# First gather of the experts as one run through four accumulator banks; gates by one product per token block

## The chip, the cores and the metric

The kernel runs on one core of one Trainium2 chip. The metric is the time on the device in microseconds of one execution. Five engines work side by side, each through its own list in its own order: TensorE (PE: matrix products; PEld is its weight load), VectorE (DVE), ScalarE (ACT), GpSimd (POOL) and SyncE (SP), which here issues the large transfers. They wait for each other by semaphores. PE writes its products into PSUM, of which this kernel uses eight pieces of 128 partitions by 2 KB, called banks here; DVE and ACT read them out into SBUF.

## What is computed

A transformer of two layers on one sequence of 256 tokens of width 1024, all in float32. Each layer is a token mixer (four kinds of attention, gated and merged), a layer norm, a mixture of 32 experts, and a second layer norm. The change lies in the mixture:

```
scores = sigmoid(x @ w_router)                     # 256 tokens, 32 experts in 8 groups of 4
g_sel  = group with the largest sum of its two best (score + bias)
e_idx  = the two best experts inside that group;  gate = their scores, normalised to sum 1
for every expert e, for the tokens sent to it:
    hid = silu(x @ w1[e]) * (x @ w3[e])            # 1024 -> 256
    y  += gate * (hid @ w2[e])                     # 256 -> 1024
x = layer_norm(ALPHA * x + y)
```

Each layer reads 32 experts of 3 MB, some 100 MB of weights.

## The kernel before

The mixture of layer `l` runs after a router. Tokens get a place in a table of 64 slots for each pair of experts; a `OH` matrix (one-hot, 256 tokens by 256 slots, made by DVE at L1260) says which token sits in which slot, for two steps of the loop at once. The main loop runs over `q` = 0 to 7 (`NQ`), and in it over `s` = 0 and 1: one `head` is a pair of experts side by side (`i` = 0, 1, each 64 slots, on the two halves of the PE columns), for `j` = 0 to 7, the eight slices of 128 of the width.

The steps that matter, with their lines:

- `gather` (L1299 to L1309): for each slice `j`, four products of x (as a high and a low part, two token blocks) with `OH` give the 256 gathered slots of that slice in PSUM, 128 by 256. DVE (L1309, even `j`) or ACT (L1307, odd `j`) scales them into `xg[:, j, :]`. Each `j` takes a PSUM tile of its own, a bank each, of a tag ("h" or "y", two banks each) that is used in turn.
- `head` (L1317): for each `j`, two products with w1 and w3 of the two experts, 64 rows by 512 columns each. The trace has two records for each product, so a head is 32 records.
- `hidden` (L1324 to L1326), `flip` (L1332 to L1334), `tail` (L1354, products with w2, read out by ACT at L1348 and DVE at L1349), `combine` (L1398 and L1394, sums into the four accumulator banks `acc`).
- `gates_of` (L1366 to L1369): the gate of each slot as a column, by a product of the one-hot with the gates of the tokens; called twice at each even `q`, after `flip_key` (L1376, read by DVE at L1379).

The first gather of a layer is special. It is interleaved with the first head: slice `j` is gathered, and from the third on the head's slice `j - 2` follows it (`GL = 2`), through the "y" banks alone. The last two slices of that head come in the loop. All later gathers run as one piece of 32 products, with "h" and "y" in turn.

The order on PE inside the loop is the order in which the code is written (`manual_schedule`); DVE, ACT and POOL are placed by the scheduler of the framework. Expert weights come through a ring of 20 slots of 1 MB (`SLOTS`), filled by SP in the order of use; a slot is loaded again when PE has finished with what it held (L1007 and L1023 issue the transfers).

Of the kernel before, what the change touches and what calls it, by code (L numbers as in the profile page):

```python
# [10 lines left out]
F32 = mybir.dt.float32  # L11
# [22 lines left out]

DS = 4
NX = 8
GL = 2
OUT_CUT = 896
HOLD = 2

# [62 lines left out]
def build(ctx, tc, I, consts, out, dbg=None, layers=L):  # L103
    nc = tc.nc
    pe, act, dve, pool = nc.tensor, nc.scalar, nc.vector, nc.gpsimd
# [12 lines left out]
    def a8(dims, dt=F32):  # L118
        t = mx.tile([128, 2048], dt, name="a8", bufs=2)
        return t.rearrange("p (a b) -> p a b", b=dims[-1])  # L120
# [251 lines left out]
    for l in range(layers):  # L372
# [25 lines left out]
        with ExitStack() as mst:  # L398
# [550 lines left out]
            for hp, u in enumerate((37 - DS, 43 - DS)):  # L949
                held, pair = {}, [None, None]  # L950
                for hh in range(2):
                    h = 2 * hp + hh
# [41 lines left out]
            a13s, a2s = {}, {}  # L994
# [40 lines left out]
            def load_ahead(n):  # L1035

                while loads and cnt[0] < n:
                    with tc.issue_after(last_load[0]):
                        loads.pop(0)()

            def release(n):
                cnt[1] += n
                load_ahead(cnt[1] + len(SLOTS))
# [16 lines left out]
            def wo_piece(n, j0):  # L1060
                return split(wos(n * 256, 256)[:, j0:j0 + 2], 2, S)
# [18 lines left out]
            with tc.issue_after(mcopy.ins):  # L1080
                for i, wt in ((1, wrb), (0, wrg[0])):
                    o = 72 + 16 * i + 8 * l
# [53 lines left out]
            for n in range(3):  # L1136
                ps = mp.tile([128, 2, S], F32, name="pj")
                for j0 in range(0, 8, 2):
                    h, lo = wop.pop(j0) if n == 0 and j0 in wop else wo_piece(n, j0)
# [7 lines left out]
            for tb in range(2):  # L1147
                ts_ = slice(tb * 128, tb * 128 + 128)
                ps = mp.tile([128, S], F32, name="pj")
                for j in range(8):  # L1150
                    if tb and j in ROUTE0:
                        route_last(0, ROUTE0.index(j))
                    h, lo = pieces[j // 2]
# [87 lines left out]
            for tb in range(2):  # L1241
                pe.matmul(prk[:, :, NP:], oneb, osel[:, tb, None, 0:NP].to_broadcast([128, 2, NP]), start=False, stop=False,
                          skip_group_check=True)
# [10 lines left out]
            G = 256  # L1254
# [12 lines left out]
            ohs = {0: oh0}  # L1267
# [16 lines left out]
            for i in range(2):  # L1284
                H = slice(64 * i, 64 * i + 64)
# [7 lines left out]
        with ExitStack() as ost:  # L1293
# [2 lines left out]

            op = ost.enter_context(tc.tile_pool(name=f"op{l}", bufs=2, space=PSUM))

            def gather(xg, oh, js, g, tags="hy"):  # L1299

                for j in js:
                    px = op.tile([128, g], F32, name=tags[j % 2])
                    for i, (xx, tb) in enumerate(((x1h, 0), (x1l, 0), (x1h, 1), (x1l, 1))):
                        pe.matmul(px, xx[:, tb, j, :], oh[:, tb, :], start=(i == 0), stop=(i == 3))  # L1304
                    g_, b_ = gpj[:, 0, l, j:j + 1], gpj[:, 1, l, j:j + 1]
                    if j % 2:
                        act.activation(xg[:, j, :], px, AF.Identity, scale=g_, bias=b_)  # L1307
                    else:
                        dve.tensor_scalar(xg[:, j, :], px, g_, b_, op0=OP.mult, op1=OP.add)  # L1309

            def head(xs, a13, ph=None, js=range(8)):

                if ph is None:
                    ph = op.tile([128, 2, 256], F32, name="h")
                for j in js:
                    for i in range(2):
                        pe.matmul(ph[64 * i:64 * i + 64], xs(j, i), a13[i][j], start=(j == 0), stop=(j == 7),  # L1317
                                  skip_group_check=True)
                return ph

            def hidden(ph, m):

                th = mx.tile([128, 256], F32, name="th", bufs=2)
                act.activation(th, ph[:, 0, :], AF.Tanh, scale=0.5)  # L1324
                dve.scalar_tensor_tensor(th, th, 1.0, ph[:, 0, :], op0=OP.add, op1=OP.mult)  # L1325
                dve.scalar_tensor_tensor(th, th, m, ph[:, 1, :], op0=OP.mult, op1=OP.mult)  # L1326
                return th
# [32 lines left out]

            def gates_of(oh, g):

                gp = op.tile([128, 1], F32, name="y")
                for tb in range(2):
                    for i in range(2):
                        pe.matmul(gp[64 * i:64 * i + 64], oh[:, tb, 64 * i:64 * i + 64].bitcast(F32), g[:, tb, i:i + 1],  # L1366
                                  start=(tb == 0), stop=(tb == 1), skip_group_check=True)
                gcol = mx.tile([128, 1], F32, name="gcol", bufs=4)
                dve.tensor_copy(gcol, gp)  # L1369
                return gcol  # L1370

            def flip_key(q):

                pt = op.tile([128, 2, 128], F32, name="y")
                for i in range(2):
                    pe.matmul(pt[64 * i:64 * i + 64], idb[0:NP, 2 * q + i:2 * q + i + 1].to_broadcast([NP, W]),  # L1376
                              keyT[0:NP], start=True, stop=True, skip_group_check=True)
                oht = mx.tile([128, S], F32R, name="oht", bufs=2)
                dve.tensor_scalar(oht, pt.rearrange("p a b -> p (a b)"), misc(2), None, op0=OP.is_equal)  # L1379
                return oht  # L1380
# [9 lines left out]
            def combine(ys, oht, first=False, final=None):  # L1390
                for fh, tb in ((0, 0), (0, 1), (1, 0), (1, 1)):
                    oh_ = oht[:, tb * 128:(tb + 1) * 128]
                    if final and fh:
                        done = pe.matmul(acc[tb][fh], oh_.bitcast(F32), ys[fh][:, 0, :], start=False, stop=False,  # L1394
                                         skip_group_check=True)
                        continue
                    for i in range(2):
                        done = pe.matmul(acc[tb][fh], oh_, ys[fh][:, i, :], start=(first and i == 0), stop=False,  # L1398
                                         skip_group_check=True)
                return done.ins  # L1400
# [23 lines left out]
            xgs = {0: a8((8, G))}  # L1424
            prev = None
            with tc.manual_schedule(engines={mybir.EngineType.PE}):
                ph = op.tile([128, 2, 256], F32, name="h")
                xs0 = lambda j, i: xgs[0][:, j, 64 * i:64 * i + 64]
                for j in range(8):
                    gather(xgs[0], ohs[0], (j,), G, "yy")  # L1430
                    if j >= GL:
                        head(xs0, a13s[0, 0], ph, (j - GL,))
                pkt = op.tile([128, 2, 128], F32, name="y")
                for tb in range(2):
                    pe.transpose(pkt[0:NP, tb, :], keyP[:, tb, :], ident)
                act.activation(keyT[0:NP], pkt[0:NP], AF.Copy)
                acc = [[op.tile([128, 512], F32, name=f"acc{tb}{fh}", bufs=1) for fh in range(2)] for tb in range(2)]
                load_ahead(len(SLOTS))
                for q in range(NQ):
                    b, o = q // 2, q % 2 * 128  # L1440
                    more = b + 1 < NQ // 2
                    ths = []
                    for s in range(2):
                        if q == s == 0:
                            head(xs0, a13s.pop((0, 0)), ph, range(8 - GL, 8))
                        else:
                            ph = head(lambda j, i: xgs[b][:, j, o + 64 * i:o + 64 * i + 64], a13s.pop((q, s)))
                        release(3 if q == 1 and s == 0 else 4)
                        ths.append(hidden(ph, mk[:, s, q:q + 1]))
                    if o and more:  # L1450
                        xgs[b + 1] = a8((8, G))
                    if prev is not None:
                        combine(*prev, first=q == 1)
                    if 2 <= q < 6:
                        xres = halves(q % 2, q // 4)
                    oht = flip_key(q)
                    if o == 0:
                        gcols = [gates_of(ohs[b][:, :, 128 * k:128 * k + 128], grP[:, :, 2 * (q + k):2 * (q + k) + 2])
                                 for k in range(2)]
                        if more:  # L1460
                            with ExitStack() if q else tc.issue_after(routed):
                                ohs[b + 1], _ = onehot(b + 1)
                    hTs = [flip(th) for th in ths]
                    if o and more:
                        gather(xgs[b + 1], ohs[b + 1], range(8), G)
                    final = q == NQ - 1
                    order = S_MAJOR if final or not q else FH_MAJOR
                    ys = tail(hTs, [a2s.pop((q, s)) for s in range(2)], gcols[q % 2], partial(b4, (2, 512)),
                              order, final)
                    release(4 if q else 2)  # L1470
                    prev = (ys, oht)
                    if 2 <= q < 6:
                        residual(*xres)
                lastc = combine(*prev, final=True)
# [135 lines left out]
```

## Time and profile before

| what | value |
|---|---|
| median of 3 runs | 1024.48 us (1021.13 to 1031.41) |
| the profiled execution | 1029.69 us, span of its instructions 1027.9 us |
| mean granted TensorE clock | 0.979 of full speed |
| PE busy | 978.0 us, 95% |
| DVE, ACT, POOL busy | 495.8, 407.5, 207.8 us |
| moved by DMA | 287.19 MB, 279 GB/s over the span |

The times of single instructions below are from the profiled execution, which took 5.2 us longer than the median of the runs. A granted clock of 1.00 is 2.4 GHz, of 0.50 is 1.2 GHz. The first gather starts at 287.77 us in layer 0 and at 795.77 us in layer 1.

### The profile page before, as it was taken

The numbers are of one execution on the slowest core, as the hardware profiler recorded it, in microseconds if no ns is written. First come the engines' busy times: TensorE is split into PE (matmuls) and PEld (weight loads), VectorE is DVE, ScalarE is ACT, GpSimd is POOL, SyncE is SP. The second block draws the span as 40 slices with busy tenths as digits, with TensorE's granted clock in tenths as the row PEclk, the third lists the DMA queues.
The fourth block names the chain that finished last, engine by engine and source line by source line (L and its number), as shares of the span: only waits on it lengthen the run. The fifth ranks groups of instructions, "written<-read, shape, count | busy, mean of one in ns | idle before, by whom it ended". The sixth has DMA issues, their size and how long they took to land. (4 is left out here: it accounts for less than half of the span.)

```text
span 1027.9 us, 16864 instructions
## 1 busy us (share of the span) xinstructions
PE 978.0 (95%) x6451; PEld 687.7 (67%) x6451; DVE 495.8 (48%) x1142; ACT 407.5 (40%) x866; POOL 207.8 (20%) x198
## 2 busy tenths in 40 slices
PE   7999999999889999999989999999997999999994
PEld 6989998999743434343487999989996343433432
DVE  4776767668632212111367766685777221111114
ACT  4756666665411212111254666666553111111111
POOL 5340124012210313000035301141214003130001
PEclk8999999999989999999999999999998999999998
DMA  9875444489679999999996454554996899999994
GB/s 285 260 227 159 150 149 148 164 286 386 236 243 373 386 387 386 386 386 386 325 308 201 127 157 133 160 163 158 331 386 204 281 381 387 387 386 386 386 386 159
DMA packets 179234, 287.19 MB, mean 279 GB/s; under 512 B 11358, under 2 KB 74596, under 8 KB 179140
## 3 DMA queue, kind: packets, MB, share of 16 engines
q1 hardware_dynamic: 177732, 282.48, 78.9%
q0 software_dynamic: 1264, 3.41, 1.3%
q8 instruction: 56, 0.92, 0.4%
q14 instruction: 38, 0.31, 0.1%
q10 hardware_dynamic: 144, 0.07, 0.0%
HBM read 284.55 MB, written 1.38 MB: 278 GB/s over the span
## 5 line engine op out<-in xcount | busy, mean ns | idle before, releaser
L420 DVE TENSOR_TENSOR b<-w,b 128x512 fp32r<-128x512 f32 (+2 forms) x294 | 214.6, 745 | 103.0 <-ACT b L415 98.6
L415 ACT ACTIVATE b<-w 128x512 fp32r<-128x512 f32 (+2 forms) x294 | 179.7, 622 | 129.8 <-PE pj L455 102.4
L453 PE MATMUL pj<-big,b 128*128 128x256 f32 x736 | 214.4, 291 | 0.8 <-DVE a L541 0.5
L455 PE MATMUL pj<-big,b 128*128 128x256 f32 x736 | 209.7, 285 | 1.3 <-DVE b L420 1.3
L454 PE MATMUL pj<-big,b 128*128 128x256 f32 x736 | 209.2, 284 | 0.0
L453 PEld LDWEIGHTS pj<-big,b 128*128 128x128 f32 x736 | 142.0, 193 | 7.1 <-issue 3.5
L455 PEld LDWEIGHTS pj<-big,b 128*128 128x128 f32 x736 | 142.0, 193 | 2.1 <-DVE b L420 2.1
L454 PEld LDWEIGHTS pj<-big,b 128*128 128x128 f32 x736 | 142.2, 193 | 0.1
L1317 PE MATMUL h<-xw,a 128*64 128x512 f32 x496 | 111.7, 597 | 0.0
L1325 DVE SCALAR_TENSOR_TENSOR th<-th,h 128x256 f32<-128x256 f32 x32 | 13.5, 421 | 180.1 <-ACT th L1324 180.1
L1324 ACT ACTIVATE th<-h 128x256 f32<-128x256 f32 x32 | 12.3, 385 | 194.9 <-PE h L1317 194.9
L1317 PE MATMUL h<-w,a 128*64 128x512 f32 x400 | 89.1, 593 | 0.0
L1317 PEld LDWEIGHTS h<-xw,a 128*64 128x64 f32 x496 | 34.3, 137 | 64.5 <-issue 61.1
L1349 DVE SCALAR_TENSOR_TENSOR b<-y,gcol,b 128x512 fp32r<-128x512 f32 x30 | 22.5, 751 | 113.2 <-ACT b L1348 113.2
L1317 PEld LDWEIGHTS h<-w,a 128*64 128x64 f32 x400 | 28.4, 137 | 56.2 <-issue 53.7
L1354 PE MATMUL y<-w,hT 128*64 128x512 f32 x256 | 57.7, 595 | 1.9 <-ACT hT L1334 1.9
L1348 ACT ACTIVATE b<-y,gcol 128x512 fp32r<-128x512 f32 x30 | 20.6, 688 | 94.7 <-PE y L1354 94.7
L546 POOL TENSOR_TENSOR R<-R,a 128x512 f32<-128x512 f32 x20 | 35.3, 1778 | 111.8 <-DVE a L541 106.3
L453 PE MATMUL pj<-b,big 128*128 128x256 f32 x192 | 55.9, 291 | 1.6 <-ACT b L415 1.3
L455 PE MATMUL pj<-b,big 128*128 128x256 f32 x192 | 55.0, 287 | 0.1
L454 PE MATMUL pj<-b,big 128*128 128x256 f32 x192 | 54.6, 285 | 0.0
L344 POOL TENSOR_TENSOR rs<-ve,mhalf 128x1 f32<-128x1 f32 (+1 forms) x6 | 4.1, 680 | 219.6 <-DVE mr L1533 160.4
(364 smaller groups left out, 1675.2 us busy)
## 6 DMA issues: line engine op xcount, KB each, us to landing
w<-in_moe_w SPq DMA_DIRECT2D x164, 512.0 KB, 10.8
xw<-in_moe_w SPq DMA_DIRECT2D x160, 512.0 KB, 10.8
w<-in_w_gate SPq DMA_DIRECT2D x32, 1024.0 KB, 5.4
w<-in_w_in SPq DMA_DIRECT2D x18, 1024.0 KB, 11.9
w<-in_w_out SPq DMA_DIRECT2D x8, 1024.0 KB, 5.0
ohl<-in_moe_w SPq DMA_DIRECT2D x16, 512.0 KB, 10.8
R<-in_moe_w SPq DMA_DIRECT2D x16, 512.0 KB, 9.9
X<-in_moe_w SPq DMA_DIRECT2D x16, 512.0 KB, 10.7
```

The costliest lines, as they stand in the source:

```text
L415: act.activation(h, v, AF.Copy)
L420: dve.tensor_sub(lo, v, h.bitcast(F32))
L453: pe.matmul(o, lh, rh, start=start, stop=False, skip_group_check=True)
L454: pe.matmul(o, lh, rl, start=False, stop=False, skip_group_check=True)
L455: return pe.matmul(o, ll, rh, start=False, stop=stop, skip_group_check=True).ins
L546: eng.tensor_tensor(merged[:, c:c + 2, :], merged[:, c:c + 2, :], tc_, op=OP.add)
L1317: pe.matmul(ph[64 * i:64 * i + 64], xs(j, i), a13[i][j], start=(j == 0), stop=(j == 7), skip_group_check=True)
L1324: act.activation(th, ph[:, 0, :], AF.Tanh, scale=0.5)
L1325: dve.scalar_tensor_tensor(th, th, 1.0, ph[:, 0, :], op0=OP.add, op1=OP.mult)
L1348: act.activation(ys[:, 0, :], py, AF.Copy, scale=gcol)
L1349: dve.scalar_tensor_tensor(ys[:, 1, :], py, gcol, ys[:, 0, :].bitcast(F32), op0=OP.mult, op1=OP.subtract)
L1354: pe.matmul(pys[fh][64 * i:64 * i + 64, :], hTs[s][:, c, 64 * i:64 * i + 64], a2[s][fh][i][:, c], start=(s == 0 and c == 0), stop=(s == le ...
```

## The change

The first gather no longer alternates with the first head. The four accumulator banks are reserved earlier, the eight slices are gathered one after the other into them, two slices to a bank (the even `j` in the first 256 columns, the odd `j` in the second), and then both heads of `q` = 0 run whole. In the odd slice the first product does not start a new sum, so that the half already written stays. In `gates_of`, for each token block one product of 128 rows by 2 columns takes the place of two of 64 rows by 1 column, and two copies of 64 rows take the diagonal blocks in place of one copy of 128 rows.

```diff
--- before.py
+++ after.py
@@ -34,7 +34,6 @@
 
 DS = 4
 NX = 8
-GL = 2
 OUT_CUT = 896
 HOLD = 2
 
@@ -1296,12 +1295,14 @@
 
             op = ost.enter_context(tc.tile_pool(name=f"op{l}", bufs=2, space=PSUM))
 
-            def gather(xg, oh, js, g, tags="hy"):
+            def gather(xg, oh, js, g, banks=None):
+
 
                 for j in js:
-                    px = op.tile([128, g], F32, name=tags[j % 2])
+                    px = banks[j // 2][:, j % 2 * g:j % 2 * g + g] if banks else op.tile([128, g], F32, name="hy"[j % 2])
                     for i, (xx, tb) in enumerate(((x1h, 0), (x1l, 0), (x1h, 1), (x1l, 1))):
-                        pe.matmul(px, xx[:, tb, j, :], oh[:, tb, :], start=(i == 0), stop=(i == 3))
+                        pe.matmul(px, xx[:, tb, j, :], oh[:, tb, :], start=(i == 0 and not (banks and j % 2)), stop=(i == 3),
+                                  skip_group_check=banks is not None)
                     g_, b_ = gpj[:, 0, l, j:j + 1], gpj[:, 1, l, j:j + 1]
                     if j % 2:
                         act.activation(xg[:, j, :], px, AF.Identity, scale=g_, bias=b_)
@@ -1360,13 +1361,13 @@
 
             def gates_of(oh, g):
 
-                gp = op.tile([128, 1], F32, name="y")
+                gp = op.tile([128, 2], F32, name="y")
                 for tb in range(2):
-                    for i in range(2):
-                        pe.matmul(gp[64 * i:64 * i + 64], oh[:, tb, 64 * i:64 * i + 64].bitcast(F32), g[:, tb, i:i + 1],
-                                  start=(tb == 0), stop=(tb == 1), skip_group_check=True)
+                    pe.matmul(gp, oh[:, tb, :].bitcast(F32), g[:, tb, :], start=(tb == 0), stop=(tb == 1))
                 gcol = mx.tile([128, 1], F32, name="gcol", bufs=4)
-                dve.tensor_copy(gcol, gp)
+                for i in range(2):
+                    H = slice(64 * i, 64 * i + 64)
+                    dve.tensor_copy(gcol[H], gp[H, i:i + 1])
                 return gcol
 
             def flip_key(q):
@@ -1424,27 +1425,19 @@
             xgs = {0: a8((8, G))}
             prev = None
             with tc.manual_schedule(engines={mybir.EngineType.PE}):
-                ph = op.tile([128, 2, 256], F32, name="h")
-                xs0 = lambda j, i: xgs[0][:, j, 64 * i:64 * i + 64]
-                for j in range(8):
-                    gather(xgs[0], ohs[0], (j,), G, "yy")
-                    if j >= GL:
-                        head(xs0, a13s[0, 0], ph, (j - GL,))
+                acc = [[op.tile([128, 512], F32, name=f"acc{tb}{fh}", bufs=1) for fh in range(2)] for tb in range(2)]
+                gather(xgs[0], ohs[0], range(8), G, acc[0] + acc[1])
                 pkt = op.tile([128, 2, 128], F32, name="y")
                 for tb in range(2):
                     pe.transpose(pkt[0:NP, tb, :], keyP[:, tb, :], ident)
                 act.activation(keyT[0:NP], pkt[0:NP], AF.Copy)
-                acc = [[op.tile([128, 512], F32, name=f"acc{tb}{fh}", bufs=1) for fh in range(2)] for tb in range(2)]
                 load_ahead(len(SLOTS))
                 for q in range(NQ):
                     b, o = q // 2, q % 2 * 128
                     more = b + 1 < NQ // 2
                     ths = []
                     for s in range(2):
-                        if q == s == 0:
-                            head(xs0, a13s.pop((0, 0)), ph, range(8 - GL, 8))
-                        else:
-                            ph = head(lambda j, i: xgs[b][:, j, o + 64 * i:o + 64 * i + 64], a13s.pop((q, s)))
+                        ph = head(lambda j, i: xgs[b][:, j, o + 64 * i:o + 64 * i + 64], a13s.pop((q, s)))
                         release(3 if q == 1 and s == 0 else 4)
                         ths.append(hidden(ph, mk[:, s, q:q + 1]))
                     if o and more:
```

How PE's list stands, first gather of layer 0, before; `big_3504` and `big_3505` are the high and low part of x, `y` and `h` PSUM tiles, and the names behind "waits" are the engines or DMA queues whose semaphore the row waits for:

```order
L1304 MATMUL y<-OH,big_3504 128x256 [waits DVE_49]
L1304 MATMUL y<-OH,big_3505 128x256 [waits Pool_49]
L1304 MATMUL y<-OH,big_3504 128x256
L1304 MATMUL y<-OH,big_3505 128x256
L1304 MATMUL y<-OH,big_3504 128x256
L1304 MATMUL y<-OH,big_3505 128x256
L1304 MATMUL y<-OH,big_3504 128x256 [waits DVE_49]
L1304 MATMUL y<-OH,big_3505 128x256
L1304 MATMUL y<-OH,big_3504 128x256
L1304 MATMUL y<-OH,big_3505 128x256
L1317 MATMUL h<-xw,a_3583 64x512 [waits DMAHW6_49,DMAHW5_49]
L1317 MATMUL h<-xw,a_3583 64x512
```

These are the second half of slice 0, slices 1 and 2, and the first slice of the head. Slice 1 starts without a wait; slice 2, which takes the bank of slice 0 again, waits for DVE. The same place now, from the second half of slice 0 on:

```order
L1304 MATMUL acc_3586<-OH,big_3504 128x256 [waits DVE_49]
L1304 MATMUL acc_3586<-OH,big_3505 128x256 [waits Pool_49]
L1304 MATMUL acc_3586<-OH,big_3504 128x256 [waits DVE_49]
L1304 MATMUL acc_3586<-OH,big_3505 128x256
L1304 MATMUL acc_3586<-OH,big_3504 128x256
L1304 MATMUL acc_3586<-OH,big_3505 128x256
L1304 MATMUL acc_3587<-OH,big_3504 128x256
L1304 MATMUL acc_3587<-OH,big_3505 128x256
L1304 MATMUL acc_3587<-OH,big_3504 128x256
L1304 MATMUL acc_3587<-OH,big_3505 128x256
L1304 MATMUL acc_3587<-OH,big_3504 128x256 [waits DVE_49]
L1304 MATMUL acc_3587<-OH,big_3505 128x256
```

Slice 1 (third row) and slice 3 (eleventh row), the second ones of their banks, now start with a wait for DVE; slice 2 (seventh row), the first one of its bank, has none. Slices 5 and 7 wait in the same way.

The gates in PE's list at `q` = 0, before, with the last product of `flip_key` ahead and the first `flip` behind:

```order
L1376 MATMUL y<-keyT,idb 64x256
L1366 MATMUL y<-grP,OH 64x1 [waits PE_49]
L1366 MATMUL y<-grP,OH 64x1 x3
L1366 MATMUL y<-grP,OH 64x1 [waits DVE_49]
L1366 MATMUL y<-grP,OH 64x1 x3
L1332 MATMUL h<-K,th 128x128 x2
```

and now:

```order
L1377 MATMUL y<-keyT,idb 64x256
L1366 MATMUL y<-grP,OH 128x2 [waits PE_49]
L1366 MATMUL y<-grP,OH 128x2
L1366 MATMUL y<-grP,OH 128x2 [waits DVE_49]
L1366 MATMUL y<-grP,OH 128x2
L1333 MATMUL h<-K,th 128x128 x2
```

Each call issues two products in place of four; the second call waits for DVE as it did.

## Rows read from the trace of the kernel before

**Rows 1.** Page: busy time of the engines (us, share of the span, instructions)

```profile
PE 978.0 (95%) x6451; PEld 687.7 (67%) x6451; DVE 495.8 (48%) x1142; ACT 407.5 (40%) x866; POOL 207.8 (20%) x198
```

**Rows 2.** Timeline of PE, layer 0 (start, duration, engine, line, tiles, count, [idle before])

```profile
287.77 3.06 PE L1304 MATMUL y<-OH,big 128*128 128x256 f32 x12
290.76 1.47 PE L1317 MATMUL h<-xw,a 128*64 128x512 f32 x4
...
300.55 0.39 PE L1435 MATMUL y<-K,keyP 128*16 128x128 f32 x2
300.87 8.80 PE L1317 MATMUL h<-xw,a 128*64 128x512 f32 x40
309.60 0.29 PE L1376 MATMUL y<-keyT,idb 16*64 16x256 bf16 x2
...
310.48 0.40 PE L1366 MATMUL y<-grP,OH 128*64 128x1 f32 x8 [0.26 <-DVE oht L1379]
310.81 0.44 PE L1332 MATMUL h<-K,th 128*128 128x128 f32 x2
```

**Rows 3.** Timeline of PE, the same place in layer 1

```profile
795.77 1.63 PE L1304 MATMUL y<-OH,big 128*128 128x256 f32 x8
797.57 0.74 PE L1304 MATMUL y<-OH,big 128*128 128x256 f32 x4 [0.16 <-DVE a L1309]
...
816.69 0.29 PE L1376 MATMUL y<-keyT,idb 16*64 16x256 bf16 x2
```

**Rows 4.** Timeline of DVE: slices read out, slice 0 of layer 0, slices 0 and 2 of layer 1

```profile
289.01 0.54 DVE L1309 TENSOR_SCALAR a<-y,gpj 128x256 f32<-128x256 f32 x1 [1.44 <-PE y L1304]
...
796.97 0.54 DVE L1309 TENSOR_SCALAR a<-y,gpj 128x256 f32<-128x256 f32 x1 [1.25 <-PE y L1304]
...
798.34 0.54 DVE L1309 TENSOR_SCALAR a<-y,gpj 128x256 f32<-128x256 f32 x1 [0.34 <-PE y L1304]
```

**Rows 5.** Timeline of PE: a later gather of layer 0, in one piece

```profile
336.08 0.73 PE L1304 MATMUL h<-OH,big 128*128 128x256 f32 x4 [0.32 <-ACT hT L1334]
336.65 0.64 PE L1304 MATMUL y<-OH,big 128*128 128x256 f32 x4
337.13 0.64 PE L1304 MATMUL h<-OH,big 128*128 128x256 f32 x4
```

**Rows 6.** Chain of waits that ended last: two heads in one piece (start, length)

```profile
963.37 13.88 PE h L1317 x64
```

**Rows 7.** Stretches: length, busy of PE, PEld, DVE, ACT, POOL, clock, DMA share, GB/s

```profile
285.30:288.10 2.80, 2.68 (x12) 1.77 (x12) 1.84 (x10) 0.20 (x1) 1.64 (x4) 0.50 1.01 349
288.20:291.50 3.30, 3.30 (x14) 2.55 (x15) 1.64 (x6) 0.56 (x1) 0.00 (x0) 0.50 0.67 244
291.60:294.00 2.40, 2.40 (x13) 0.90 (x10) 0.00 (x0) 0.56 (x1) 0.00 (x0) 1.00 0.02 3
793.40:796.70 3.30, 3.20 (x15) 2.30 (x15) 1.83 (x10) 0.20 (x1) 1.64 (x4) 0.50 0.96 333
520.30:523.60 3.30, 2.28 (x20) 2.28 (x20) 1.15 (x3) 1.31 (x3) 0.09 (x1) 1.00 0.95 188
```

**Rows 8.** Timeline of PE: products of 128 rows by 1 column elsewhere

```profile
30.81 1.40 PE L673 MATMUL tp<-K,a 128*128 128x1 f32 x12
32.07 0.36 PE L453 MATMUL pj<-big,b 128*128 128x256 f32 x1
```

**Rows 9.** Timeline of SP: first expert weights issued again, layer 0

```profile
293.94 0.88 SPq L1023 DMA_DIRECT2D xw<-in_moe_w  x2
```

**Rows 10.** Stretches, as in rows 7: DMA later in layer 0, and at the end of layer 1

```profile
340.00:345.00 5.00, 5.00 (x26) 1.77 (x26) 0.73 (x2) 1.25 (x2) 2.54 (x2) 1.00 1.03 379
1010.00:1015.00 5.00, 5.00 (x20) 2.00 (x16) 2.51 (x4) 1.38 (x2) 0.00 (x0) 1.00 0.05 15
```

**Rows 11.** Timeline of PE: the last tail of layer 1

```profile
1005.42 7.09 PE L1354 MATMUL y<-w,hT 128*64 128x512 f32 x32 [0.32 <-ACT hT L1334]
```

## The prediction, made before the changed kernel ran

> **What bounds the kernel now.** I read the page's engine table first: PE is busy for 978.0 of 1027.9 us, 95%, and no other engine for half of it [rows 1]. Then the timeline of PE around the first gather of each layer, because all that the change moves on the critical engine lies there. In layer 0 PE works from 287.77 us (first product of the gather) to 309.60 (`flip_key`, after the second head) without a gap between the rows [rows 2]; in layer 1 from 795.77 to 816.69 with one gap of 0.16 us [rows 3]. So a microsecond of PE saved or lost there is a microsecond of the layer, unless a later wait takes it up. Third, the clock that PE was granted: the gather begins at 0.50 in both layers. In layer 0 it stays so through 288.20 to 291.50 and reads 1.00 from 291.60 on; in layer 1 it is 0.50 up to 796.70 [rows 7], and the products behind that run at full speed. So part of the gather is paid at half speed, and how long depends on when the clock rises.
>
> **What the change removes.** Six slices of the head no longer alternate with the gather. Before, from 290.76 to 300.55 in layer 0, PE did six head slices and five gather slices in 9.79 us [rows 2]. In one piece a gather slice takes 0.48 us (336.65 to 337.13) [rows 5] and a head slice, four records, 13.88 / 16 = 0.87 us [rows 6]: 5 x 0.48 + 6 x 0.87 = 7.6 us. Some 2 us per layer are the price of changing between the two, part of it at the slow clock.
>
> **What it adds: a wait in every bank.** The order of the changed program shows that slices 1, 3, 5 and 7 start with a wait for DVE, and slices 2, 4 and 6 do not. DVE reads out the even slices, so the second half of a bank is written only after the first half has been read. Four times per layer PE stands still while DVE reads 256 columns. The trace of before has one such wait, though at another place: in layer 1 DVE reads slice 0 from 796.97 for 0.54 us [rows 4], and PE, whose slice 2 wants that bank, goes on at 797.57 [rows 3], 0.06 us after the read ended. The way from PE to DVE is 0.03 us: four products from 797.57 last 0.74 us, to 798.31 [rows 3], and DVE starts at 798.34 [rows 4].
>
> The Trainium skill (PSUM — Partial Sum Buffer, "PSUM bank collisions raise a hardware error") says the same of this from the chip's side: PE writing and another engine reading one bank at once is an error even at different columns, so the guard goes by bank. By that page packing two slices into a bank buys no overlap between them; no run here shows what happens without the guard. The sum without that wait is the third rival below.
>
> *Layer 1, clock as before.* DVE reads slice 0 from 796.97 as it did, PE starts slice 1 at 797.57. From there a bank costs: the odd slice, first after a wait, 0.57 (336.08 to 336.65); the next even slice to its end 0.64 [rows 5]; 0.03, 0.54 and 0.06 for the way, the read and the way back: 1.84 us. Three banks lead to 803.09, the last odd slice to 803.66, the two transposes of `keyP` (300.55 to 300.87 [rows 2]) to 803.98, two heads of 64 records [rows 6] to 817.86. Before it was 816.69 [rows 3]: **1.2 us later**.
>
> *Layer 0, clock rising at 291.55 as before.* DVE reads from 289.01 to 289.55 [rows 4], PE restarts at 289.61. At the slow clock twelve products took 2.99 us (287.77 to 290.76 [rows 2]), 0.25 each, so slice 1 ends its issue at 290.6 and slice 2 at 291.6, with its last product through at about 291.8. Read-out and ways (0.63) give 292.43, two more banks (3.68) 296.11, then 0.57 + 0.32 + 13.88 as above: 310.88 against 309.60, **1.3 us later**.
>
> **The gates.** A call before is eight records, 0.33 us to the next row (310.48 to 310.81 [rows 2]). The changed call is four records with 128 rows and 2 columns. The nearest row is L673, 128 rows by 1 column: twelve in 1.26 us (30.81 to 32.07), 0.105 each [rows 8], so 0.42 us, 0.09 more. There are sixteen calls (two at each of four values of `q`, two layers). The first of each pair hides: the second waits 0.26 us for DVE's read of `flip_key` anyway [rows 2], and goes on when that is done. The second stands on the path: 8 x 0.09 = **0.7 us**. Bounds: 0.04 per record as in the old form would give 8 x (0.16 - 0.33) = -1.4 us; twice the price taken gives +1.4 for the extra alone. The extra copies on DVE (one per call) lie beside the flips; DVE's copy is needed only when the tail reuses that bank, and if that cover went it would be 16 short copies.
>
> **The clock, which is the large term.** The waits make PE pause just where it must earn its clock. Before, the clock rose about 6.3 us after PE started again in layer 0 (285.3 to 291.55, nearly without a pause: 2.68 of 2.80 us busy and then 3.30 of 3.30) and about 3.4 us after in layer 1 (793.4 to 796.7, 3.20 of 3.30 busy) [rows 7]. The first wait of the changed gather falls at about 289.0 in layer 0 and 796.9 in layer 1. In layer 1 that is after the rise; in layer 0 it is before, and PE would then pause 0.6 us in every bank. If the clock does not rise amid such pauses, a bank costs at half speed 1.24 (287.77 to 289.01) + 0.54 + 0.06 + four products at 0.25 = 2.84 us; four banks lead to 299.1, the transposes at half speed to 299.7. Unbroken work begins with slice 7 at 298.1; with the 3.4 to 6.3 us of before the clock rises at 301.5 to 304.4, so 1.8 to 4.7 us of the heads go at half speed and cost half of that again. End: 299.7 + 13.88 + (0.9 to 2.35) = 314.5 to 315.9, that is 4.9 to 6.3 us later than before; for a layer 1 that loses its early rise, 508.0 us further on, 5.8 to 7.2 us later. I take **6.0 us** for a layer in which the clock is late, in place of 1.2.
>
> That the clock falls again in the gather once it is up is unlikely: 520.30 to 523.60 has PE busy for 2.28 of 3.30 us, with the clock at 1.00 [rows 7], about the share that the gather with waits has (1.21 of 1.84). The Trainium skill (TensorE: Matmul & The Clock Gate, "Loop structure matters more than you think") lists dense products with DVE's copy from PSUM between them among the loops that keep the clock. The trace agrees for a clock that is up; for one that has still to rise no row here shows it. If the page held there too, the first rival would be the outcome.
>
> **Sum.** One layer late, as the profiled execution's own times suggest: 6.0 + 1.2 + 0.7 = +7.9 us. On the profiled execution (1029.69) that is 1037.6; it lies 5.2 us above the median of 1024.48, to which the forecast refers: **1032.4 us**, +0.8%.
>
> **Rivals.**
>
> 1. *The clock rises as before in both layers.* For it: the pauses are short. Then only the waits and the gates count: 1.2 + 1.3 + 0.7 = +3.2, 1027.7 us. Chance 0.27.
> 2. *The clock is late in both layers.* For it: the moment of the rise differed by 2.9 us between two layers with the same order of work, so the 3.4 us of layer 1 may have been luck that another execution lacks. 12.0 + 0.7 = +12.7, 1037.2 us. Chance 0.29.
> 3. *PE does not stand still* (the read of a half is over before PE gets to the other half, or the wait is met early), and the gather runs at its 0.48 us per slice. It decides at 0.16 us: only if DVE's 0.63 us of way and read shrank below what PE pipelines anyway. Layer 0: 17 products left at 291.6, x 0.12 = 2.0, + 0.32 + 13.88 gives 307.8, 1.8 earlier; layer 1: 28 left at 796.7 give 814.3, 2.4 earlier; with the gates -3.5, 1021.0 us, not slower. Against it speaks the order. Chance 0.06.
> 4. *The expert weights become the bound.* The first slot of the ring is freed when head slice 1 is done, in layer 0 at 297.0 + 1.7 = 298.7 in place of 293.94 [rows 9], and later the queues are full (share 1.03 at 379 GB/s [rows 10]). The last quarter of the last tail starts at 1005.42 + 5.3 = 1010.7 [rows 11], and DMA is quiet from 1010 on (share 0.05 [rows 10]); so the margin is about a microsecond or two. If transfers slip by more than PE does, 1 to 2 us per layer come on top of any case above: 1034 to 1036 on the forecast. As a bound of its own I give it 0.04.
>
> The forecast keeps 0.34.
>
> **How the numbers follow.** The range holds forecast and rivals 1, 2 and 4: from rival 1 less the gates' lower bound and some scatter, 1024.5, to rival 2 with DMA's microseconds on top, 1040.0. One per cent, about what this kernel's measurement can tell from no change, is 1034.7 upwards and 1014.2 downwards. Slower by more than that: most of rival 2 (0.25), a part of the forecast and of rival 4 (0.09): 0.34. Faster by more than 1%: no case reaches it; 0.02. Within 1%: 0.64.
>
> **What would show it.** In the timeline of PE, eight gather rows of four products with a wait "<- DVE a" of some 0.6 us before slices 1, 3, 5 and 7; a gap there of 0.1 us or none is rival 3. In the granted clock, whether 0.50 lasts beyond the gather, in which layer. The heads as one row of 64 records, some 13.9 us where the clock is up. At L1366, four records per call and the distance from the second call to the flip, 0.42 us. Idle time of PE before L1354 in the last tail, put down to a DMA, would be rival 4. I am wrong in the mechanism if the gather shows no waits, and in the size if the clock does otherwise than said.

## The result and the profile after

The changed kernel took 1034.92 us in the median of 12 runs (1032.42 to 1039.27), the kernel before 1025.79 us (12 runs, 1021.13 to 1031.41): 9.1 us more, a ratio of 1.0101 with a 95% interval of 1.0085 to 1.0118; the quotient of the two medians, 1.0089, lies in it. The forecast was 1032.4 us, the range 1024.5 to 1040. The profiled execution took 1039.21 us, with a span of 1037.4 us and a mean clock of 0.971.

Line numbers are shifted by a few: the gather is still L1304, its read-out by DVE L1310, the head L1318, `flip_key` L1377, the gates L1366, the flip L1333, the tail L1355, the transposes of `keyP` L1432. The page's row of busy times answers to [rows 1]:

```profile
PE 987.9 (95%) x6387; PEld 696.7 (67%) x6387; DVE 496.7 (48%) x1158; ACT 406.9 (39%) x866; POOL 209.9 (20%) x198
```

PE is busy for 9.9 us more with 64 instructions fewer. A larger sum over fewer instructions asks for the clock. The timeline of PE in layer 0, which answers to [rows 2]:

```profile
287.89 1.20 PE L1304 MATMUL acc<-OH,big 128*128 128x256 f32 x4
289.72 2.08 PE L1304 MATMUL acc<-OH,big 128*128 128x256 f32 x8 [0.64 <-DVE a L1310]
292.44 2.07 PE L1304 MATMUL acc<-OH,big 128*128 128x256 f32 x8 [0.64 <-DVE a L1310]
295.15 2.08 PE L1304 MATMUL acc<-OH,big 128*128 128x256 f32 x8 [0.64 <-DVE a L1310]
297.87 1.22 PE L1304 MATMUL acc<-OH,big 128*128 128x256 f32 x4 [0.64 <-DVE a L1310]
298.89 0.63 PE L1432 MATMUL y<-K,keyP 128*16 128x128 f32 x2
299.45 16.32 PE L1318 MATMUL h<-xw,a 128*64 128x512 f32 x64
315.70 0.29 PE L1377 MATMUL y<-keyT,idb 16*64 16x256 bf16 x2
315.93 1.26 PE L1366 MATMUL y<-grP,OH 128*128 128x2 f32 x8
317.05 0.41 PE L1333 MATMUL h<-K,th 128*128 128x128 f32 x2
```

Four rows begin with a wait of 0.64 us for DVE: slices 1, 3, 5 and 7. A bank comes round every 2.72 us (289.72 to 292.44). DVE's timeline says what PE waits for, as in [rows 4]: the read of slice 0 ends at 289.66, PE goes on at 289.72; the read of slice 2 ends at 292.39, PE goes on at 292.44.

```profile
289.12 0.54 DVE L1310 TENSOR_SCALAR a<-acc,gpj 128x256 f32<-128x256 f32 x1 [1.45 <-PE acc L1304]
...
291.84 0.55 DVE L1310 TENSOR_SCALAR a<-acc,gpj 128x256 f32<-128x256 f32 x1 [1.45 <-PE acc L1304]
```

The same place in layer 1, against [rows 3]:

```profile
798.38 1.20 PE L1304 MATMUL acc<-OH,big 128*128 128x256 f32 x4
800.21 2.08 PE L1304 MATMUL acc<-OH,big 128*128 128x256 f32 x8 [0.64 <-DVE a L1310]
...
809.93 15.38 PE L1318 MATMUL h<-xw,a 128*64 128x512 f32 x64
825.24 0.29 PE L1377 MATMUL y<-keyT,idb 16*64 16x256 bf16 x2
```

In neither layer are the two heads done in the 13.88 us of [rows 6]. The stretches around the gathers (columns as in [rows 7]) say why:

```profile
285.40:288.90 3.50, 3.36 (x15) 2.35 (x14) 1.85 (x10) 0.20 (x1) 1.63 (x4) 0.50 1.00 348
289.00:304.10 15.10, 12.54 (x43) 7.92 (x44) 2.83 (x8) 2.52 (x5) 0.00 (x0) 0.50 0.10 39
304.40:306.00 1.60, 1.60 (x10) 0.56 (x8) 0.00 (x0) 0.00 (x0) 0.00 (x0) 1.00 0.84 262
...
799.60:812.70 13.10, 10.57 (x38) 7.35 (x40) 2.83 (x8) 2.51 (x5) 0.00 (x0) 0.50 0.12 45
813.00:815.00 2.00, 2.00 (x12) 0.70 (x10) 0.00 (x0) 0.00 (x0) 0.00 (x0) 1.00 0.28 31
```

The clock stays at 0.50, its lower level of 1.2 GHz, through the whole gather with its pauses and into the heads. Before, it read 1.00 from 291.60 on in layer 0 and was up after 796.70 in layer 1 [rows 7].

The span cut into stages (us, from the first row of one to the first row of the next; "out" is the last combine) shows where the 9.5 us between the two profiled spans lie. The last row is a second profile of the kernel before, from the experiments:

| | to gather 0 | gather and two heads | rest of the experts | out and mixer 1 | gather and two heads | rest | end | span |
|---|---|---|---|---|---|---|---|---|
| before | 287.77 | 21.83 | 196.80 | 289.37 | 20.92 | 196.79 | 14.42 | 1027.9 |
| after | 287.89 | 27.81 | 197.58 | 285.10 | 26.86 | 197.74 | 14.42 | 1037.4 |
| difference | +0.12 | +5.98 | +0.78 | -4.27 | +5.94 | +0.95 | 0.00 | +9.5 |
| before, second profile | 286.14 | 21.38 | 196.78 | 285.44 | 20.90 | 196.78 | 14.48 | 1021.9 |

The -4.27 is no gift of the change. In the first profile of before, PE idled more and the clock was also low at the start of layer 1's mixer, where the change does nothing; in the second profile that stage took 285.44. The first row is the first profile, the second row the second one:

```profile
510.00:521.00 11.00, 7.58 (x39) 6.76 (x38) 6.29 (x13) 4.75 (x9) 2.31 (x4) 0.84 0.64 209
510.00:521.00 11.00, 9.29 (x73) 8.59 (x72) 7.91 (x18) 7.34 (x16) 1.16 (x2) 1.00 0.77 204
```

The first profile was an execution 5.2 us above its median, as the prediction said; this is where most of that lay.

### The profile page after: what moved, and what is told of

Its sections match the earlier page's. It is cut to its first block, busy times and chain, and to the rows that moved or that the text cites. A ratio compares the mean times of both kernels' runs of the same rounds, so it can differ in the third digit from the quotient of the medians.

```text
span 1037.4 us, 16758 instructions
## 1 busy us (share of the span) xinstructions
PE 987.9 (95%) x6387; PEld 696.7 (67%) x6387; DVE 496.7 (48%) x1158; ACT 406.9 (39%) x866; POOL 209.9 (20%) x198
## 5 line engine op out<-in xcount | busy, mean ns | idle before, releaser
L1318 PE MATMUL h<-xw,a 128*64 128x512 f32 x496 | 112.5, 610 | 0.0
L1326 DVE SCALAR_TENSOR_TENSOR th<-th,h 128x256 f32<-128x256 f32 x32 | 13.5, 421 | 193.2 <-ACT th L1325 193.2
L1318 PE MATMUL h<-w,a 128*64 128x512 f32 x400 | 89.1, 593 | 0.2 <-DMA w<-in_moe_w 0.2
L1318 PEld LDWEIGHTS h<-xw,a 128*64 128x64 f32 x496 | 36.1, 141 | 73.1 <-issue 70.5
L1318 PEld LDWEIGHTS h<-w,a 128*64 128x64 f32 x400 | 28.4, 137 | 56.7 <-issue 52.1
L1355 PE MATMUL y<-w,hT 128*64 128x512 f32 x256 | 57.7, 595 | 1.9 <-ACT hT L1335 1.9
```

The costliest lines, as they stand in the source:

```text
L1355: pe.matmul(pys[fh][64 * i:64 * i + 64, :], hTs[s][:, c, 64 * i:64 * i + 64], a2[s][fh][i][:, c], start=(s == 0 and c == 0), stop=(s == le ...
```

## The experiments

My theory: the pauses keep a low clock from rising, and that, not the new gates, is the loss. Rivals: the gates cost it; or it lies in having the gather in one piece. "Below" and "above" are against the kernel before on the same chip, worked out from the ratio; the intervals are at 95%. A late layer is one whose clock is still low through its whole gather; "gather and heads" is the time from the first product of the gather to `flip_key`.

**Even slices first.** Each bank is still shared by two slices, but the second half is written long after the first was read.

```diff
-                gather(xgs[0], ohs[0], range(8), G, acc[0] + acc[1])
+                gather(xgs[0], ohs[0], (0, 2, 4, 6, 1, 3, 5, 7), G, acc[0] + acc[1])
```

> The change with one thing altered: the first gather takes the slices in the order 0, 2, 4, 6, 1, 3, 5, 7, so each bank is read out while PE fills the other three. Theory (the pauses at the second slice of each bank, and the slow clock that comes with them, are the loss): no wait of PE for DVE inside the gather, the gather at 0.48 us per slice once the clock is up, first product to flip_key some 20 us in layer 0 (27.8 in the changed kernel, 21.8 before), clock up within 3.4 to 6.9 us of the restart of PE; time 2 to 3 us below the kernel before, about 1023 us, 11 to 12 below the change. Rival 'losing the interleaving is the loss' (heads and with them the expert weights start later): stays 6 us or more above the kernel before. Rival 'the gates are the loss': stays 8 or more above.

Measured: 1023.39 us, ratio 0.9994 (0.9981 to 1.0006). The timeline of PE in layer 0 has the gather in one row, without a wait:

```profile
285.25 4.46 PE L1304 MATMUL acc<-OH,big 128*128 128x256 f32 x32
289.55 0.38 PE L1432 MATMUL y<-K,keyP 128*16 128x128 f32 x2
289.86 13.95 PE L1318 MATMUL h<-xw,a 128*64 128x512 f32 x64
303.74 0.29 PE L1377 MATMUL y<-keyT,idb 16*64 16x256 bf16 x2
...
306.34 5.35 PE L1355 MATMUL y<-b,hT 128*64 128x512 f32 x16
```

Against the changed kernel this one order saves some 11 us (1.0101 less 0.9994, of 1024): the pauses are the loss. Gather and heads take 18.49 and 19.46 us, 2.9 and 1.4 less than in the second profile of before. But the time came out only 0.6 us below before, not resolved, and not 2 to 3. One place of return is in the last row: the first tail, 16 products, takes 5.35 us in place of 3.65. The stretch shows the clock falling again after the gather:

```profile
303.70:306.60 2.90, 2.38 (x18) 1.67 (x18) 2.43 (x9) 0.92 (x3) 0.00 (x0) 1.00 1.04 392
306.70:310.00 3.30, 3.30 (x10) 0.98 (x8) 0.00 (x0) 0.13 (x1) 0.00 (x0) 0.50 1.05 389
310.10:312.00 1.90, 1.90 (x12) 0.63 (x10) 0.00 (x0) 0.00 (x0) 0.00 (x0) 1.00 1.02 374
```

**The old gates.** The changed kernel with `gates_of` as before.

```diff
-                gp = op.tile([128, 2], F32, name="y")
+                gp = op.tile([128, 1], F32, name="y")
                 for tb in range(2):
-                    pe.matmul(gp, oh[:, tb, :].bitcast(F32), g[:, tb, :], ...)
+                    for i in range(2):
+                        pe.matmul(gp[64 * i:64 * i + 64], oh[:, tb, 64 * i:64 * i + 64].bitcast(F32), g[:, tb, i:i + 1], ...)
                 gcol = mx.tile([128, 1], F32, name="gcol", bufs=4)
-                for i in range(2):
-                    H = slice(64 * i, 64 * i + 64)
-                    dve.tensor_copy(gcol[H], gp[H, i:i + 1])
+                dve.tensor_copy(gcol, gp)
```

> The change with the old gates (two products of 64 rows by 1 column per token block, one copy), the gather as changed. Theory: the gates cost 0.13 us in each of eight places, 1.0 us together; time some 8 us above the kernel before, one below the change. Rival 'the gates are the loss': within 2 us of the kernel before.

Measured: 1037.56 us, ratio 1.0116 (1.0095 to 1.0137). That is some 12 us above before, where 8 were expected; the loss is still there whole. The profile has the four waits of 0.64 us in both layers and both layers late, with 26.72 and 27.48 us for gather and heads. What the gates cost is too small for this comparison; the traces give it below.

**Work for PE in the pauses.** One product of the identity, 256 columns, behind each even slice; its result is not used.

```diff
-                gather(xgs[0], ohs[0], range(8), G, acc[0] + acc[1])
+                fill = op.tile([128, 256], F32, name="h")
+                for j in range(8):
+                    gather(xgs[0], ohs[0], (j,), G, acc[0] + acc[1])
+                    if j % 2 == 0:
+                        pe.matmul(fill..., ident, ident..., start=True, stop=True, ...)
```

> The change with one identity product of 256 columns more (result unused) behind each even slice of the first gather, that is inside the pause; the wait for DVE stays where it is. Theory (the pauses cost 1.2 us per layer, the clock that does not rise amid them the other 4 to 5): the clock rises within 7 us of PE's restart in both layers, the gather is done some 9 to 10 us after its start, not 11; first product to flip_key 22 to 24 us in each layer, in place of 27; time 3 to 5 us above the kernel before. If the clock has its own reasons (the waits alone cost the 6 us): 0.50 lasts to the heads as in the changed kernel, and the time is 9 to 12 us above.

Measured: 1028.72 us, ratio 1.0042 (1.0029 to 1.0056), 4.3 us above. PE's timeline and two stretches in layer 0:

```profile
287.46 1.48 PE L1304 MATMUL acc<-OH,big 128*128 128x256 f32 x8
288.78 0.60 PE L1433 MATMUL h<-K 128*128 128x256 f32 x2
289.58 1.22 PE L1304 MATMUL acc<-OH,big 128*128 128x256 f32 x8 [0.20 <-DVE a L1310]
...
308.05 0.29 PE L1377 MATMUL y<-keyT,idb 16*64 16x256 bf16 x2
```

```profile
285.60:288.00 2.40, 2.37 (x8) 1.90 (x9) 1.07 (x5) 0.00 (x0) 0.15 (x1) 0.50 0.93 344
288.10:294.00 5.90, 5.29 (x35) 4.01 (x34) 1.66 (x4) 1.70 (x3) 0.00 (x0) 1.00 0.05 19
```

PE still goes on with an odd slice only when DVE has read the even one, and yet gather and heads take 22.4 us in both layers in place of 27.8 and 26.9: the clock reads 1.00 from 288.10 on in layer 0, and it is up early in layer 1 too. So 4.5 to 5.4 us of a late layer's 6 are the clock alone. This is the experiment that parts the clock from the wait.

**One run through the old banks.** The kernel before, with the interleaving taken out and all eight slices gathered through "h" and "y" in turn as later gathers do; accumulator banks and gates untouched.

```diff
-                for j in range(8):
-                    gather(xgs[0], ohs[0], (j,), G, "yy")
-                    if j >= GL:
-                        head(xs0, a13s[0, 0], ph, (j - GL,))
+                gather(xgs[0], ohs[0], range(8), G)
```

> The kernel before with only the interleaving taken out: the first gather is one run through the four banks of the tags h and y in turn, one slice to a bank, as all later gathers are; old gates. Theory: no pause, six or more changes between gather and head saved, 1.8 us in layer 0 and 2.4 in layer 1, time 3 to 4 us below the kernel before. Rival 'losing the interleaving is the loss': 5 us or more above.

Measured: 1024.26 us, ratio 0.9988 (0.9974 to 1.0003): not resolved, where 3 to 4 us were expected. Yet gather and heads are as short as hoped, 19.31 and 18.81 us. Two things take back a part. In layer 1 the first tail lies at the low clock again; and in layer 0 PE's last head now waits for its weights, which it hardly did before:

```profile
490.05 1.94 PE L1317 MATMUL h<-w,a 128*64 128x512 f32 x8 [0.71 <-DMA w<-in_moe_w]
```

**The changed kernel with the clock held up.** PE runs products with no other use ahead of the gather, `NW1` of them (L305); 22 in place of 8 fill its idle time there.

```diff
-NW1 = 8
+NW1 = 22
```

> The change with 22 in place of 8 identity products (results unused) ahead of the router's last step, so that PE works through the 6.9 us for which it otherwise idles; the gather as changed, waits and all. Theory (of the 6 us per layer some 1.2 are the waits, the rest the clock that does not rise amid them): clock at 1.00 through the gather, the four waits still there at about 0.6 us, first product to flip_key 21.6 us in place of 27, the gather some 0.5 us earlier; time 9 to 12 us below the change, within 2 us of the kernel before. If the waits alone cost 6 us per layer: still 8 us or more above the kernel before. If the clock falls in the gather although it was up: 0.50 again at some 3 us into it.

Measured: 1027.74 us, ratio 1.0045 (1.0032 to 1.0058). PE's timeline of layer 0 and the stretch of the gather:

```profile
286.86 0.73 PE L1304 MATMUL acc<-OH,big 128*128 128x256 f32 x4
288.23 1.21 PE L1304 MATMUL acc<-OH,big 128*128 128x256 f32 x8 [0.64 <-DVE a L1310]
290.07 1.21 PE L1304 MATMUL acc<-OH,big 128*128 128x256 f32 x8 [0.64 <-DVE a L1310]
...
294.65 13.95 PE L1318 MATMUL h<-xw,a 128*64 128x512 f32 x64
308.53 0.29 PE L1377 MATMUL y<-keyT,idb 16*64 16x256 bf16 x2
```

```profile
287.00:294.60 7.60, 5.04 (x34) 4.04 (x34) 3.40 (x14) 1.76 (x4) 0.75 (x3) 1.00 0.44 153
```

The same four pauses of 0.64 us, PE busy for 5.04 of 7.60 us, and the clock stays at 1.00. A bank takes 1.84 us, gather and heads 21.67 and 21.70, as expected. By the ratios the time came down by some 6 us (from 1.0101 or, in the second measurement further down, 1.0109) and not by 9 to 12. The expectation had taken the first profile of the changed kernel for its usual case, with both layers late; against its second profile the two stages save 0.5 and 4.4 us, most of what the time shows. It is also still 4.6 us above before, where at most 2 were expected. Against the second profile of before, gather and heads account for 1.1 us of that and the rest of the experts (197.56 and 197.68 against 196.78 twice) for 1.7; the remainder is not found.

**Even slices first, the old gates; and that with 22 products ahead; and the kernel before with 22.** The edits are those above together.

> The even slices first and the old gates. Theory: as the kernel with the even slices first, less 8 x 0.13 = 1 us for the gates; 1 to 3 us below the kernel before, ratio 0.997 to 0.999. If the new gates cost nothing: the same as the kernel with the even slices first, 0.999.

> Even slices first, old gates, and 22 products in the idle time ahead: no pause and no slow clock. Theory: gather 3.9 us, first product to flip_key 18.1 us in both layers, the gather 0.5 us earlier; some 6 to 8 us below the kernel before, ratio 0.992 to 0.994, the first version that beats both. Rival 'the expert weights are next': PE is ready earlier than the last weights, idle time of PE put down to DMA of 1 to 4 us per layer before the last tails, ratio 0.995 or more.

> The kernel before with 22 products in the idle time ahead, gather interleaved as it was. Theory: what the slow clock costs the kernel before: first product to flip_key 20 us in both layers, in place of 20.9 and 21.8, the gather 0.5 us earlier; 2 to 4 us below the kernel before, ratio 0.996 to 0.998. If the products in the idle time cost something elsewhere (they hold up the router's products, or PE's clock later on): no gain or a loss.

Measured, in this order: 1023.42 us, ratio 0.9998 (0.9983 to 1.0013); 1023.17 us, 0.9986 (0.9973 to 0.9999); 1026.21 us, 1.0023 (1.0008 to 1.0038). All three missed what was expected of the time, though the place itself did as expected in the last two: gather and heads 18.10 us in both layers, and 20.49 in both. Some returns are those seen already. The first has gather and heads at 19.26 and 19.50 us, and the wait for weights in both layers, 0.40 us in layer 0 and in layer 1:

```profile
995.54 1.94 PE L1318 MATMUL h<-w,a 128*64 128x512 f32 x8 [0.77 <-DMA w<-in_moe_w]
```

The third has the low clock in the first tail of both layers (PE's timeline):

```profile
308.13 5.35 PE L1354 MATMUL y<-b,hT 128*64 128x512 f32 x16
...
816.95 5.35 PE L1354 MATMUL y<-b,hT 128*64 128x512 f32 x16
```

Twice 1.7 us are lost there against 0.9 and 0.4 won in the gathers. But this profile is of the slowest of its seven runs, 1029.18 us, with a span 5.5 us above that of the second profile of before, and the largest part of that lies elsewhere: the stage "out and mixer 1" took 289.84 us against 285.44, with PE idle and the clock low at its start, as in the first profile of before:

```profile
510.00:521.00 11.00, 6.21 (x32) 5.53 (x31) 4.58 (x10) 4.16 (x9) 1.45 (x3) 0.69 0.85 229
```

So what makes the median 1.0023 is not shown. In the other two that stage took 287.64 and 287.14 us, a return of some 2 us each that no expectation had. The second is the best version there is: 1.4 us below before, with an interval that hardly leaves out no change.

**Both kernels profiled again**, to see whether the clock at the gather differs between executions.

> The kernel before, unaltered, for a second profile. Theory (the first profile lay 5 us above the median because of the clock outside the gather): first product to flip_key again 20.5 to 22.5 us per layer; the way from layer 1's start to its gather nearer 276 than 279.8 us; total within 2 us of 1024.5. If the gather is where executions of this kernel differ: less than 20.5 in a layer.

> The changed kernel, unaltered, for a second profile and a ratio on another chip. Theory: four waits of 0.64 us in each gather; a layer whose clock rises before the first wait takes 22 to 23 us from first product to flip_key, one whose clock does not takes 26 to 28; one or two of the two layers are of the second kind; ratio 1.008 to 1.012. If the late clock of both layers in the first profile was an accident: both layers 22 to 23 us, ratio about 1.004.

The kernel before: 1023.66 us, gathers and heads 21.38 and 20.90. The changed kernel: 1035.32 us, ratio 1.0109 (1.0085 to 1.0134). Its profile has layer 0 early and layer 1 late. PE's timeline of both, then the stretches:

```profile
289.52 1.22 PE L1304 MATMUL acc<-OH,big 128*128 128x256 f32 x8 [0.64 <-DVE a L1310]
...
309.86 0.29 PE L1377 MATMUL y<-keyT,idb 16*64 16x256 bf16 x2
...
796.42 2.08 PE L1304 MATMUL acc<-OH,big 128*128 128x256 f32 x8 [0.64 <-DVE a L1310]
...
820.73 0.29 PE L1377 MATMUL y<-keyT,idb 16*64 16x256 bf16 x2
```

```profile
282.00:288.70 6.70, 3.36 (x15) 2.35 (x14) 4.95 (x23) 1.00 (x2) 3.14 (x5) 0.50 0.66 223
288.80:292.00 3.20, 1.92 (x14) 1.64 (x14) 1.74 (x6) 0.56 (x1) 0.00 (x0) 1.00 0.49 183
790.60:807.50 16.90, 12.72 (x49) 9.32 (x50) 6.16 (x22) 2.71 (x6) 2.31 (x5) 0.50 0.37 125
```

The same program, the same order: where the clock was up by 288.80, before PE took up slice 1 at 289.52, the gather runs at full speed with its pauses and the stage takes 22.17 us; where it was not, 26.14 us.

## Why the prediction was right, and where it was off

**The wait in every bank** held in place and size. Expected were waits before slices 1, 3, 5 and 7 of 0.03 + 0.54 + 0.06 = 0.63 us; they are 0.64 everywhere. A bank was put at 1.84 us with the clock up and took 1.84 (288.23 to 290.07 with the clock held up); at the low clock at 2.84 and took 2.72, since the eight products and the way to DVE took 2.12 us (289.72 to 291.84) where the sum had 2.24. The third rival (PE does not stand still) is out. With the clock up at both kernels' gathers the stage is 21.67 - 20.49 = 1.2 us longer, the forecast's figure for layer 1. That is the net of the waits and of what the one run saves; against the one run without waits, clock up (18.10), the waits alone cost 3.6 us, 0.88 a bank (1.84 against twice the 0.48 of [rows 5]).

**The clock** was the large term, and 6.0 us per late layer was right: +5.98 and +5.94. The clock read 0.50 up to 304.10 and 1.00 from 304.40, the late end of the 301.5 to 304.4 that was given; in layer 1, 510.5 us further on, it rose between 812.70 and 813.00, near the early end. That 6.0 came out within 0.1 us is in part luck: the five late layers of three profiles took 26.14 to 27.81 us, 5.2 to 6.6 more than the same layer in the second profile of before. The reason given was right too: with the pauses filled the clock rose at 288.1, and with the clock up beforehand the same pauses left it up. How often it is late was the open question, and the forecast's one late layer was a choice between two near chances. The first profile of the changed kernel has both layers late, which is the second rival (+12.7); the second has one, the forecast (+7.9); the one with the old gates has both. That is five layers of six, against none of the twelve layers where the pauses are absent or filled and no more than 8 products run ahead. The medians, 9.1 and 10.5 us above before, lie between the two cases, and the twelve runs reach from 6.6 to 13.5 above the median of before. Four of them have a mean clock of 0.971 and 1038.9 to 1039.3 us, as the first profile has; the other eight have 0.973 to 0.979 and 1032.4 to 1036.4 us, and the second profile had 0.977. That fits a mixture, with both cases frequent; it does not sort every run, since the profile with the old gates had both layers late at 0.973. The first rival as a whole, +3.2 in most executions, is out.

The Trainium skill (TensorE: Matmul & The Clock Gate, "Loop structure matters more than you think") counts DVE's copies out of PSUM among what leaves dense products warm. The gather with the clock held up agrees, 5.04 of 7.60 us busy at 1.00, though the products in the skill's loop follow at once and here they wait for the copy. The stretch 289.00 to 304.10, 12.54 of 15.10 us busy at 0.50, lies outside what that section says, because there the clock had still to rise.

**The gates** were mis-sized. The step that failed is the price of 0.105 us for a product of 128 rows and 2 columns, from L673 [rows 8]. The second call of a pair starts at 316.57, when DVE has read what `flip_key` wrote (its read ends at 316.52), and its four records last to the flip at 317.05: 0.48 us, 0.12 each, where 0.42 were expected. From `flip_key` to the flip it is 1.35 us (315.70 to 317.05), against 1.21 before (309.60 to 310.81 [rows 2]): 0.14 at each of eight places, 1.1 us in all against 0.7. That the first call of a pair hides was right: the second starts 0.87 us after `flip_key` starts (315.70 to 316.57), as it did before (0.88, 309.60 to 310.48).

**Interleaving's price** was put at some 2 us per layer and is at least that: with the pauses gone and the clock up in both, gather and heads take 18.10 against 20.49 us, 2.4 less. The prediction let the waits eat it, and they did.

**The expert weights** (fourth rival) do not bound the changed kernel; its rest of the experts grew by 0.78 and 0.95 us, and four places of gates are 0.56 of each. One wait for weights of 0.22 us stands in layer 1. Where the gather is faster, the rival appears: of the eight layers with gather and heads under 20 us, four wait 0.27 to 0.77 us at the last head. Of the four that do not, three had lost 1.7 us in the first tail.

**What stays open.** Why the clock falls in the first tail in some executions (5.35 in place of 3.65 us) and not in others. In the twelve profiles of this case, with two layers each, it happened six times: even slices first in layer 0, one run through the old banks and the best version in layer 1, the kernel before with 22 products in both, and the changed kernel's second profile in layer 0. It never came behind a late clock at the gather, but not behind each early one either. Nothing here separates a cause from chance, and with it the 3 us or so that the traces promise and the times don't give are accounted for in part only. Open too is why "out and mixer 1" took 287.1 to 289.8 us in four of the twelve profiles (the first of before, and the three kernels told of together above) and 284.3 to 286.6 in the others.

## What to carry to other kernels

Two results in one PSUM bank that another engine reads made a wait per bank here; with all first halves written before any second half the wait was gone, at no cost that the traces show. Price such a pause twice: by what a bank takes longer, 0.88 us here for a pause of 0.64, and by the clock it falls under, since the same four pauses, less what the one run saves, cost 1.2 us with the clock up and 6 us where it had still to rise. And look at where a stage's gain can be given back before counting it: here the weights took a part in some layers, and a low clock in the first tail in others.

## What was not expected of the hardware

A pause of 0.64 us in each 2.72 us kept the clock at 0.50 for some 15 us more with PE busy for 12.54 of 15.10 us, while at 1.00 pauses of 0.64 in each 1.84 us, busy for 5.04 of 7.60 us, did not bring it down. Elsewhere it fell behind short sparse work, without a cause being shown: with the even slices first, flips and gates with PE busy for 2.38 of 2.90 us were followed by 3.3 us at 0.50, in full work, and the first tail behind them was slow in six of 24 layers. Filling PE's idle time ahead of the gather gave a clock of 1.00 there, and the kernel before still took 2.4 us longer with it. Records of 128 rows and 2 columns of float32 took 0.12 us each in the gates, against 0.105 with 1 column [rows 8] and 0.04 for the old gates' 64 rows and 1 column.
